# Issuing the stores of the recurrences from POOL's queue instead of SP's in a hybrid HGRN2 / Mamba-2 layer

## The chip, the cores and the metric

The kernel runs on one core of a Trainium2 chip. The core has five engines that work side by side, each through its own instructions in order: TensorE (PE, matrix products; its weight loads are shown as PEld), VectorE (DVE), ScalarE (ACT), GpSimd (POOL) and SyncE (SP). SP computes nothing; it issues DMA transfers. POOL computes and can issue DMA transfers too. An issued transfer runs on the core's 16 DMA engines; its issuer goes on to its next instruction. Engines wait for each other and for transfers through semaphores.

The metric is device time in microseconds (us), the median of several runs. Less is better.

## What is computed

One layer of a decoder trunk for two request groups that share all weights: a prompt of 1024 tokens from a zero state, and 8 sample tokens with states of their own. All data is fp32, the model width is 1024.

```python
h = rmsnorm(x, norm1_w)
q, f, i, g, z, xbc, dt = split(h @ w_in)            # 1024 -> 6672 columns
# A: HGRN2, 8 heads, key and value dim 128
f = lb + (1 - lb) * sigmoid(f); k = 1 - f; q = silu(q)
S = f_t * S + k_t v_t;  o = q_t S                   # chunked over the prompt; one step per sample
o_a = rmsnorm(o) * silu(g)
# B: Mamba-2 SSD, 16 heads of 64, 2 B/C groups, state 128
X, B, C = silu(causal_conv4(xbc)); dt = softplus(dt + bias)
S = exp(A dt) * S + dt X B;  y = C S + D X
y = rmsnorm(y * silu(z))
x = x + concat(o_a, y) @ w_out                      # 2048 -> 1024
gate, val = split(rmsnorm(x, norm2_w) @ w_up)       # 1024 -> 2 x 2816
x = x + (silu(causal_conv3(gate)) * val) @ w_down
y = rmsnorm(x, final_norm_w)
```

Returned are y and the new states of both groups: HGRN states, SSM states, the last rows before each convolution.

## The kernel before, in words

A token column set holds 1024 prompt tokens and 8 sample tokens (NT = 1032) and is cut into three chunks of 344 columns for the input projection. Each fp32 product is made of three: a tile is split into a high part (rounded on ScalarE) and a low part (the rest, by a subtraction on VectorE), and TensorE adds high·high, high·low and low·high. So a weight tile of 128 columns, 512 KB, is loaded by SP into `ws` (two buffers, L182), cast on ScalarE (L183) and subtracted on VectorE (L184).

The input projection is a list of **jobs** (`in_job`), one for each 128 columns, each of 72 matrix products. Between the products of the jobs the program interleaves the work of the recurrences, by `drive(stream, weight, name)`: the stream yields numbers, and for each so many matrix products of the jobs are issued. Weights are loaded two jobs ahead. **TensorE's order is written out by hand** (`manual_schedule` for PE alone); the order of VectorE, ScalarE, POOL and SP is made when the program is built, by a scheduler that estimates when each instruction can run. Each of these engines then works in that fixed order.

In order of time:

- norm of the input, first columns of B and C, dt (about 0 to 100 us);
- SSM recurrence of group 0, `ssd(0)`, then of group 1, in 8 chunks of 128 tokens. `ssd_front` (L519) loads rows of decay sums (`csb`), makes B's transpose (`bt`), X·dt (`xdt`, L543, VectorE) and its decayed form (`xde`, L544, POOL). `ssd_back` (L549) makes the output and the next state: `ecs` (loaded; L563 on VectorE), the decayed state (L568, POOL), its sum with the new part (L569, VectorE), output sums (L579, L582). TensorE needs the state of L569 for the next chunk's product `yo`;
- `ssm_decode` (L614), one step for the samples, in two halves of four samples for each of eight head pairs: it loads B and C rows (`Bb`, `Cb`) and the state `Sd` (two buffers), scales it on ScalarE (L627), multiplies on VectorE (L628), adds (L629), **stores the state (L630)**, multiplies by C on POOL (L631) and reduces on VectorE (L632), then updates the sample columns (L633);
- `ssm_gate` (L642): jobs z, whose columns gate the SSM output; `tail` (L679) scales the four tiles of a group (L683) and **stores them in the scratch tensor `mix_d` (L684)**;
- eight HGRN heads (`head`, L810). The sample rows of v are **stored in scratch `vd_d` (L824)** and loaded back as `vb`, broadcast; the sample states `Sh` are loaded, updated on VectorE and POOL (L833 to L835) and **stored (L836)**, and used by TensorE (`od`). Levels of products with `f`, `k`, `q`, `v` follow (L853 to L857), the prompt state is **stored (L948)**, the output is normed (L983, POOL) and **stored in `mix_d` (L988)**;
- beside them, rows before the convolution go out through a buffer `csr` (**L698, L699**), and one DRAM to DRAM copy (**L700**); the prompt's SSM state goes out through `so` (**L597**);
- the output projection: the rows of `mix_d` are loaded back as `ml` (`mix_load`, L1001), split (L998 on ScalarE, L999 on VectorE), multiplied; evictions in ScalarE (L1038) or VectorE (L1040). Residual input columns `xs` are loaded by `residual_load` (L756), in buffers that `vb` uses too;
- from about 1000 us on: second norm, up projection, down projection, final norm. None of the changed lines lies there.

All loads and all stores named here are issued by SP, in one order. POOL issues only nine small loads (`vec`, L139) at the start.

Changed and calling functions:

Of the kernel before, what the change touches and what calls it, by code (L numbers as in the profile page):

```python
# [20 lines left out]
NT = T + ND  # L21
# [29 lines left out]
def hybrid_layer(  # L51
# [9 lines left out]
    V, A, G, PE, SP = nc.vector, nc.scalar, nc.gpsimd, nc.tensor, nc.sync  # L61
# [27 lines left out]
    def bank(s, tag="mx"):  # L89
        return psmx.tile([P, 512], F32, tag=tag, bufs=NBANK[tag], name=nm(s))  # L90
# [237 lines left out]
    mix_d = dram.tile([16, P, NT], F32, name="mix_d")  # L328
# [96 lines left out]
    for i in range(9):  # L425
        n = P if i < 8 else ND
# [164 lines left out]
    def ssm_state_out(g):  # L591
        ps = bank("sT")
        for i in range(4):
            PE.transpose(ps[:, i * P:(i + 1) * P], S[g][:, i * P:(i + 1) * P], ident)
        so = half("so")
        V.tensor_copy(so, ps)
        SP.dma_start(ssm_prompt[0, 0, g * 8:(g + 1) * 8].rearrange("(i h) p n -> (h p) i n", h=2),  # L597
                     so.rearrange("p (i n) -> p i n", n=P))

    def d4(t):  # L600
        return t.rearrange("p (b n) -> p b n", n=P)
# [12 lines left out]
    def ssm_decode(g, i):  # L614
        j = g * 4 + i
        xdd = small.tile([P, 2, ND], F32, tag="xdd", name=nm("xdd"))
        xdec = Xg[g][i][:, T:NT]
        V.tensor_tensor(xdd[:, 0, :], xdec, ddb[:, 0, j, :], op=ALU.mult)
        for b0 in (0, 4):
            bs = slice(b0, b0 + 4)  # L620
            Bb, Cb = tl("d", "Bb")[:, :512], tl("d", "Cb")[:, :512]
            for t_, r in ((Bb, 2 * g), (Cb, 2 * g + 1)):
                fetch(t_, bc_d[r, bs].rearrange("b n -> (b n)").unsqueeze(0).to_broadcast([P, 512]))
            Sd = tl("ld", "Sd")
            fetch(d4(Sd), state_ssm[0, bs, 2 * j:2 * j + 2].rearrange("b h p n -> (h p) b n"))
            for b in range(4):
                A.activation(d4(Sd)[:, b, :], d4(Sd)[:, b, :], AF.Copy, scale=ddb[:, 1, j, b0 + b:b0 + b + 1])  # L627
            V.tensor_tensor(d4(Bb), d4(Bb), cb(xdd[:, 0, bs]), op=ALU.mult)  # L628
            V.tensor_tensor(Sd, Sd, Bb, op=ALU.add)  # L629
            SP.dma_start(ssm_sample[0, bs, 2 * j:2 * j + 2].rearrange("b h p n -> (h p) b n"), d4(Sd))  # L630
            G.tensor_tensor(Cb, Sd, Cb, op=ALU.mult)  # L631
            V.tensor_reduce(xdd[:, 1, bs], d4(Cb), axis=mybir.AxisListType.X, op=ALU.add)  # L632
        V.scalar_tensor_tensor(xdec, xdec, d_bc[:, j:j + 1], xdd[:, 1, :], op0=ALU.mult, op1=ALU.add)  # L633
# [8 lines left out]
    def ssm_gate(g):  # L642
        acc = []

        def z_job(i):
            j = g * 4 + i

            def begin():
                if i == 0:
                    acc.append(tl("g", "gacc"))  # L650
                if g:
                    ssm_decode(1, i)
                elif i < 2:
                    ssm_decode(0, i + 2)

            def evict(c, cs, ps):
                Y = Xg[g][i][:, cs]
                sz = tl("z", "sz")[:, :CH]
                A.activation(sz, ps, AF.Silu)
                V.tensor_tensor(Y, Y, sz, op=ALU.mult)  # L660
                if i == 0:
                    A.activation(acc[0][:, cs], Y, AF.Square)
                else:
                    A.activation(sz, Y, AF.Square)
                    (V if g or i == 3 else G).tensor_tensor(acc[0][:, cs], acc[0][:, cs], sz, op=ALU.add)
                if i == 3:
                    after(36 + 14 * g, lambda: rstd(c))
            in_job(f"z{j}", OFF_Z + j * P, evict, begin=begin)

        def rstd(c):  # L670
            cs = chunks[c]
            ps = bank("ms", "nx")
            mm(ps[:, :CH], ones, acc[0][:, cs])
            rstd_of(acc[0][:, cs], tl("z", "nt")[:, :CH], ps[:, :CH], 512)

            if c == NCH - 1:
                tail()

        def tail():  # L679
            for i in range(4):  # L680
                j = g * 4 + i
                Y = Xg[g][i][:, :NT]
                V.scalar_tensor_tensor(Y, Y, col("sn", j), acc[0][:, :NT], op0=ALU.mult, op1=ALU.mult)  # L683
                SP.dma_start(mix_d[8 + j], Y)  # L684

        for i in range(4):
            z_job(i)

    def ssm_conv_state():
        for j0 in range(0, XT, 4):  # L690
            yield
            ps = bank("l11", "nx")
            for j in range(4):
                PE.transpose(ps[:11, j * P:(j + 1) * P], last11[:, j0 + j, :], ident)
            csr = keep.tile([16, 512], F32, tag="csr", bufs=1, name=nm("csr"))
            V.tensor_copy(csr[:11, :512], ps[:11, :])
            cl = slice(j0 * P, (j0 + 4) * P)
            SP.dma_start(cs_prompt[0, 0, :, cl], csr[0:3, :512])  # L698
            SP.dma_start(cs_sample[0, :, 2, cl], csr[3:11, :512])  # L699
        SP.dma_start(cs_sample[0, :, 0:2, :], state_conv_ssm[0, :, 1:3, :])  # L700

    def ssd(g):
        parts = {}
# [36 lines left out]
    vd_d = dram.tile([H, ND, P], F32, name="vd_d")  # L740
# [69 lines left out]
    def head(h, t):  # L810
        f, k, q, v, sg = (t[n] for n in ("f", "k", "q", "v", "sg"))
# [9 lines left out]
            A.copy(vt[hf], ps)  # L821
        vd = small.tile([ND, P], F32, tag="vd", name=nm("vd"))
        V.tensor_copy(vd, dps[:ND, :P])
        SP.dma_start(vd_d[h], vd)  # L824
        V.tensor_tensor(qb[:, :, 0:ND], eye8, q[:, T:NT].unsqueeze(2).to_broadcast([P, ND, ND]), op=ALU.mult)
        Sds = []
        for b0 in (0, 4):
            bs = slice(b0, b0 + 4)
            ds = slice(T + b0, T + b0 + 4)
            Sd, vb = tl("ld", "Sh"), tl("d", "vb")[:, :512]  # L830
            fetch(d4(Sd), state_hgrn[0, bs, h].rearrange("b k v -> k b v"))
            fetch(vb, vd_d[h, bs].rearrange("b n -> (b n)").unsqueeze(0).to_broadcast([P, 512]))
            G.tensor_tensor(d4(vb), d4(vb), cb(k[:, ds]), op=ALU.mult)  # L833
            V.tensor_tensor(d4(Sd), d4(Sd), cb(f[:, ds]), op=ALU.mult)
            G.tensor_tensor(Sd, Sd, vb, op=ALU.add)  # L835
            SP.dma_start(hgrn_sample[0, bs, h].rearrange("b k v -> k b v"), d4(Sd))  # L836
            Sds.append(d4(Sd))


# [80 lines left out]
        for b in range(ND):  # L920
            g = b % 4
# [12 lines left out]
        Sprev, before = None, []  # L934
        for hf in range(2):
# [4 lines left out]
            for i in range(4):  # L940
# [4 lines left out]
                    V.scalar_tensor_tensor(SS[hf][:, blk[i]], Sprev, Tc[:, hf * 4 + i:hf * 4 + i + 1], ps[:, blk[i]],  # L945
                                           op0=ALU.mult, op1=ALU.add)
                Sprev = SS[hf][:, blk[i]]
        SP.dma_start(hgrn_prompt[0, 0, h], Sprev)  # L948
        dps = bank("odp", "nx")
        mm(dps[:, :ND], odr, selod)  # L950
        od = small.tile([P, 3, ND], F32, tag="dsq", name=nm("od"))
# [6 lines left out]
        for hf in range(2):  # L958
            oh = sg[:, hb[hf]]
            ps = bank("o")  # L960
            for i in range(4):
                n = hf * 4 + i
# [22 lines left out]
        oh = sg[:, T:NT]  # L985
        V.scalar_tensor_tensor(oh, od[:, 0, :], col("hn"), oh, op0=ALU.mult, op1=ALU.mult)
        V.tensor_tensor(oh, oh, od[:, 1, :], op=ALU.mult)
        SP.dma_start(mix_d[h], sg[:, :NT])  # L988


    def split(src, hi, lo):
# [409 lines left out]
    for c in (3, 0, 1, 2):  # L1401
# [4 lines left out]
        for t0 in range(cs.start, cs.stop, P):  # L1406
            n = min(P, cs.stop - t0)
# [49 lines left out]
```

## Time and profile before

| | |
|---|---|
| median of 3 runs | 1786.03 us (1785.04 to 1788.24) |
| profiled execution | 1782.61 us, span 1780.9 us |
| granted clock of TensorE, mean | 0.991 |
| TensorE busy | 1725.4 us, 97% |
| VectorE busy | 1119.3 us, 63% |
| ScalarE busy | 817.5 us, 46% |
| transfers issued by SP (hardware queue) | 179.80 MB, 32.3% of 16 engines' span |
| transfers issued by POOL (software queue) | 0.10 MB |

The profile is of one execution. Busy time counts instructions on an engine; issuing a DMA isn't counted, but shown in the timeline. A row of the waits reads "engine, line <- what released it: us in total, times, longest". A row of the timeline reads start, length (us), engine, line, operation, output<-inputs, shape, count, and in brackets the idle time before it and what ended it; rows with a count above 1 are merged, and a length is then that of the whole. A row of the stage table reads stretch, its length, then busy time of PE, PEld, DVE, ACT and POOL with counts, the granted clock of TensorE (1.00 is full), the DMA engines' share and GB/s.

### The profile page before, as it was taken

To read this page: it belongs to the slowest core of one execution; us is meant where nothing else is said; L and a number is where in the kernel's file an instruction comes from. 1 tells how busy PE (TensorE), PEld (TensorE's weight loads), DVE (VectorE), ACT (ScalarE), POOL (GpSimd) and SP (SyncE) were. 2 spreads that over 40 slices of the span, in tenths; PEclk is the share of its full clock that TensorE was granted. 3 is DMA by queue.
4 is the path that set the end of the run, shared out by engine and by line. 5 is a ranking of instruction groups with operands and counts; after the bars stand their busy time and mean duration, and the time that the engine had idled before them with its cause. 6 is when DMAs were issued, how large, how long until landed. Compare 5 with 4: busy or idle time off the path is not lost. (4 is left out here: it accounts for less than half of the span.)

```text
span 1780.9 us, 38506 instructions
## 1 busy us (share of the span) xinstructions
PE 1725.4 (97%) x16143; PEld 1675.6 (94%) x16143; DVE 1119.3 (63%) x2011; ACT 817.5 (46%) x1464; POOL 405.3 (23%) x415
## 2 busy tenths in 40 slices
PE   7999899999999999999999978999999999999998
PEld 6998799999999999999899978999999999999997
DVE  6667966575564565458645768666666666445545
ACT  7677688455554454545333435334333344111114
POOL 2113331220110111011000364554445542000001
PEclk9999999999999999999999998999999999999999
DMA  4144634642221222234334432222222225422212
GB/s 154 39 126 126 189 106 132 184 137 98 87 66 51 86 73 78 58 109 155 101 108 133 135 90 72 72 72 78 82 91 72 72 84 203 152 81 90 97 61 96
DMA packets 218019, 182.34 MB, mean 102 GB/s; under 512 B 13388, under 2 KB 195158, under 8 KB 217830
## 3 DMA queue, kind: packets, MB, share of 16 engines
q1 hardware_dynamic: 217558, 179.80, 32.3%
q8 instruction: 126, 2.06, 0.5%
q14 instruction: 47, 0.39, 0.1%
q0 software_dynamic: 288, 0.10, 0.0%
HBM read 141.53 MB, written 38.52 MB: 101 GB/s over the span
## 5 line engine op out<-in xcount | busy, mean ns | idle before, releaser
L93 PE MATMUL mm<-hh,wh 128*128 128x344 f32 x1248 | 405.3, 325 | 0.3 <-issue 0.2
L93 PE MATMUL mm<-hl,wh 128*128 128x344 f32 x1248 | 404.5, 324 | 0.0
L93 PE MATMUL mm<-hh,wl 128*128 128x344 f32 x1248 | 402.0, 322 | 0.0
L93 PEld LDWEIGHTS mm<-hh,wh 128*128 128x128 f32 x1248 | 235.0, 189 | 3.9 <-issue 2.6
L93 PEld LDWEIGHTS mm<-hl,wh 128*128 128x128 f32 x1248 | 235.2, 189 | 2.4 <-issue 0.9
L93 PEld LDWEIGHTS mm<-hh,wl 128*128 128x128 f32 x1248 | 235.3, 189 | 2.2 <-issue 1.5
L183 ACT CAST wh<-ws 128x1024 fp32r<-128x1024 f32 x96 | 100.5, 1047 | 242.8 <-PE dn L93 135.3
L93 PE MATMUL ub<-ul,wh 128*128 128x258 f32 x704 | 200.4, 285 | 4.3 <-DVE ul L1144 4.3
L93 PE MATMUL ub<-uh,wh 128*128 128x258 f32 x704 | 200.3, 285 | 2.0 <-ACT uh L1143 2.0
L93 PE MATMUL ub<-uh,wl 128*128 128x258 f32 x704 | 200.2, 284 | 0.0
L93 PE MATMUL dn<-ah,wh 128*128 128x256 f32 (+1 forms) x640 | 181.1, 283 | 1.2 <-DVE x L1387 1.2
L93 PE MATMUL dn<-al,wh 128*128 128x256 f32 (+1 forms) x640 | 180.6, 282 | 0.0
L93 PE MATMUL dn<-ah,wl 128*128 128x256 f32 (+1 forms) x640 | 180.2, 282 | 0.0
L184 DVE TENSOR_TENSOR wl<-ws,wh 128x1024 fp32r<-128x1024 f32 x96 | 126.4, 1317 | 72.4 <-ACT wh L183 71.4
L93 PE MATMUL mm<-mh,wh 128*128 128x258 f32 x512 | 147.7, 288 | 11.2 <-DVE x L1040 8.3
L93 PE MATMUL ua<-ul,wh 128*128 128x258 f32 x528 | 149.4, 283 | 0.9 <-DVE ul L1144 0.9
L93 PE MATMUL ua<-uh,wh 128*128 128x258 f32 x528 | 149.2, 283 | 0.0
L93 PE MATMUL ua<-uh,wl 128*128 128x258 f32 x528 | 148.4, 281 | 0.0
L93 PE MATMUL mm<-ml,wh 128*128 128x258 f32 x512 | 145.8, 285 | 0.7 <-DVE ml L999 0.7
L93 PE MATMUL mm<-mh,wl 128*128 128x258 f32 x512 | 145.9, 285 | 0.0
L93 PEld LDWEIGHTS ub<-ul,wh 128*128 128x128 f32 x704 | 134.5, 191 | 5.0 <-DVE ul L1144 5.0
L93 PEld LDWEIGHTS ub<-uh,wh 128*128 128x128 f32 x704 | 134.0, 190 | 2.5 <-ACT uh L1143 2.5
(347 smaller groups left out, 3942.8 us busy)
## 6 DMA issues: line engine op xcount, KB each, us to landing
ws<-in_w_in_dram SPq DMA_DIRECT2D x52, 512.0 KB
ws<-in_w_up_dram SPq DMA_DIRECT2D x44, 512.0 KB
ws<-in_w_out_dram SPq DMA_DIRECT2D x24, 512.0 KB
act_d<-val SPq DMA_DIRECT2D x22, 516.0 KB
al<-act_d SPq DMA_DIRECT2D x22, 516.0 KB
ws<-in_w_down_dram SPq DMA_DIRECT2D x22, 512.0 KB
ml<-mix_d SPq DMA_DIRECT2D x48, 172.0 KB
csb<-cs_d SPq DMA_DIRECT2D x32, 256.0 KB
```

Source lines behind the costliest of these rows:

```text
L93: PE.matmul(out, lhsT, rhs, start=start, stop=stop)
L183: A.copy(wh[:, :n], ws[:, :n])
L184: V.tensor_tensor(wl[:, :n], ws[:, :n], wh[:, :n].bitcast(F32), op=ALU.subtract)
```

## The change

Ten statements that store results now use POOL's queue (`G.dma_start`) instead of SP's (`SP.dma_start`). They issue 73 transfers. All loads stay with SP; so do the stores of the second half of the kernel. Source, destination and size of each transfer are unchanged. As the scheduler orders the engines anew, instructions on VectorE, ScalarE, POOL and SP change places too, mainly between 140 and 380 us and near 840 us; TensorE's order is the same.

```diff
 def ssm_state_out(g):
-        SP.dma_start(ssm_prompt[0, 0, g * 8:(g + 1) * 8].rearrange("(i h) p n -> (h p) i n", h=2),
+        G.dma_start(ssm_prompt[0, 0, g * 8:(g + 1) * 8].rearrange("(i h) p n -> (h p) i n", h=2),
                      so.rearrange("p (i n) -> p i n", n=P))
 def ssm_decode(g, i):
             V.tensor_tensor(Sd, Sd, Bb, op=ALU.add)
-            SP.dma_start(ssm_sample[0, bs, 2 * j:2 * j + 2].rearrange("b h p n -> (h p) b n"), d4(Sd))
+            G.dma_start(ssm_sample[0, bs, 2 * j:2 * j + 2].rearrange("b h p n -> (h p) b n"), d4(Sd))
             G.tensor_tensor(Cb, Sd, Cb, op=ALU.mult)
 def tail():
-                SP.dma_start(mix_d[8 + j], Y)
+                G.dma_start(mix_d[8 + j], Y)
 def ssm_conv_state():
-            SP.dma_start(cs_prompt[0, 0, :, cl], csr[0:3, :512])
-            SP.dma_start(cs_sample[0, :, 2, cl], csr[3:11, :512])
-        SP.dma_start(cs_sample[0, :, 0:2, :], state_conv_ssm[0, :, 1:3, :])
+            G.dma_start(cs_prompt[0, 0, :, cl], csr[0:3, :512])
+            G.dma_start(cs_sample[0, :, 2, cl], csr[3:11, :512])
+        G.dma_start(cs_sample[0, :, 0:2, :], state_conv_ssm[0, :, 1:3, :])
 def head(h, t):
-        SP.dma_start(vd_d[h], vd)
+        G.dma_start(vd_d[h], vd)
...
-            SP.dma_start(hgrn_sample[0, bs, h].rearrange("b k v -> k b v"), d4(Sd))
+            G.dma_start(hgrn_sample[0, bs, h].rearrange("b k v -> k b v"), d4(Sd))
...
-        SP.dma_start(hgrn_prompt[0, 0, h], Sprev)
+        G.dma_start(hgrn_prompt[0, 0, h], Sprev)
...
-        SP.dma_start(mix_d[h], sg[:, :NT])
+        G.dma_start(mix_d[h], sg[:, :NT])
```

## The prediction

> **What bounds the kernel now.** I read the page's busy table first, then TensorE's waits from 100 to 1000 us (the stretch in which all moved stores lie), then a table by stage.
>
> ```profile
> PE 1725.4 (97%) x16143; PEld 1675.6 (94%) x16143; DVE 1119.3 (63%) x2011; ACT 817.5 (46%) x1464; POOL 405.3 (23%) x415
> ```
> ```profile
> PE xp L541 <- DVE ecs L563: 3.0, 2, 2.2
> PE mm L93 <- ACT x L1038: 2.8, 1, 2.8
> PE yo L93 <- DVE S L569: 2.6, 1, 2.6
> PE a L93 <- DVE q L854: 2.5, 1, 2.5
> ```
> ```profile
> 500.00:800.00 300.00, 299.10 (x3997) 289.16 (x3996) 165.37 (x300) 149.91 (x237) 41.95 (x30) 1.00 0.26 77
> 206.20:209.40 3.20, 2.96 (x10) 2.21 (x10) 3.20 (x5) 1.28 (x4) 2.35 (x2) 0.50 0.17 45
> 411.00:414.20 3.20, 2.94 (x132) 2.83 (x133) 2.58 (x5) 0.94 (x3) 0.00 (x0) 0.50 0.59 167
> 851.30:854.50 3.20, 3.20 (x50) 2.91 (x49) 1.70 (x4) 3.08 (x10) 0.00 (x0) 0.50 0.17 52
> ```
>
> TensorE is the bound: 97% busy, and from 500 to 800 us 299.10 of 300 us. TensorE's order is the same in both kernels, so the change can only fill or open gaps. The four longest waits in the stretch make 10.9 us. The last three rows (columns: span, PE, PEld, DVE, ACT, POOL, then granted clock) show a second price: after each of the waits of 2.6, 2.5 and 2.8 us the granted clock is 0.50 for some 3.2 us, so 1.6 us is lost on top; after the wait of 2.2 us it isn't. POOL, where the stores go, is 23% busy. None of TensorE's waits here ends on a DMA or on SP, so a shorter SP queue helps only through VectorE or ScalarE.
>
> **What leaves SP.** 73 stores: 16 of the SSM decode states (L630), 16 of the HGRN decode states (L836), 16 of gate rows (L684, L988), 8 HGRN states (L948), 8 value rows (L824), 7 of convolution rows (L698 to L700), 2 SSM states (L597). SP issues in order, so a store that waits for its producer holds back the loads behind it:
>
> ```profile
> SPq L836 <- POOL Sh L835: 62.8, 16, 6.9
> SPq L630 <- DVE Sd L629: 28.2, 12, 7.4
> ```
>
> These waits go, but most are late for nobody: the loads behind them fetch weights two jobs ahead, and TensorE waits for no weight. What is late next in SP's queue is a weight load waiting for its buffer. I count a gain only where a TensorE gap follows from such a load or from the order that changes with it.
>
> **What a store costs on POOL.** No store was issued there; the small loads of the start are the nearest rows.
>
> ```profile
> L139 POOL DMA_DIRECT2D vrows<-in_norm_w_dram x2 | 1.2, 598 | 0.8 <-POOLq L1445 0.8
> L139 POOL DMA_DIRECT2D vrows<-in_ffn_conv_w_dram x1 | 0.6, 550 | 0.0
> L139 POOL DMA_DIRECT2D vrows<-in_hgrn_norm_w_dram x1 | 0.5, 511 | 0.0
>   DMA to landing us min/median/max: 4.3/5.6/6.1
> ```
> ```profile
> 147.76 3.23 POOL L544 TENSOR_TENSOR xde<-xdt,dec 128x512 f32<-128x512 f32 x1 [1.08 <-DVE xdt L543]
> 151.95 2.51 POOL L631 TENSOR_TENSOR Cb<-Sd,Cb 128x512 f32<-128x512 f32 x2
> 160.21 1.04 POOL L544 TENSOR_TENSOR xde<-xdt,dec 128x512 f32<-128x512 f32 x1 [5.74 <-DVE xdt L543]
> ```
>
> One row of 128 floats took 511 ns, 66 rows 550 ns: 0.5 us and about 0.6 to 1 ns a row. A decode-state store has 512 rows of 512 bytes, so 0.8 to 1.0 us; I take 1.0. The low end is 0.5 us. The high end is 3.2 us, what a POOL instruction of 1.04 us became when VectorE worked beside it. 73 times 1.0 us is 73 us on an engine idle for 1375 us, so POOL's total is no matter; what stands behind a store is. At L630 that is L631 (Cb), for which VectorE's L632 waits. Landing is 5.6 us after issue by these rows; on SP the value rows were stored and loaded back within 1.9 us:
>
> ```profile
> 385.51 0.31 SPq L824 DMA_DIRECT2D vd_d<-vd  x1
> 387.40 1.04 SPq L175 DMA_DIRECT2D vb<-vd_d  x2
> 404.46 3.93 SPq L684 DMA_DIRECT2D mix_d<-xbc  x4
> ```
> ```profile
> 407.23 1.28 ACT L799 ACT_TABLE_LOAD   x1 [2.12 <-DMA mix_d<-xbc]
> ```
>
> **Stage 1, the SSM recurrence of group 0 (100 to 230 us).** The change also moves instructions on VectorE and ScalarE.
>
> ```profile
> 148.80 1.29 DVE L629 TENSOR_TENSOR Sd<-Sd,Bb 128x512 f32<-128x512 f32 x2
> 153.28 0.69 DVE L632 TENSOR_REDUCE xdd<-Cb 128x4 f32<-128x512 f32 x1 [3.19 <-POOL Cb L631]
> 155.10 0.68 DVE L563 TENSOR_TENSOR ecs<-yo,ecs 128x512 f32<-128x512 f32 x1
> 176.56 0.68 DVE L629 TENSOR_TENSOR Sd<-Sd,Bb 128x512 f32<-128x512 f32 x1
> 184.37 0.67 DVE L632 TENSOR_REDUCE xdd<-Cb 128x4 f32<-128x512 f32 x1
> 184.96 1.16 DVE L629 TENSOR_TENSOR Sd<-Sd,Bb 128x512 f32<-128x512 f32 x1
> 186.04 1.53 DVE L628 TENSOR_TENSOR Bb<-Bb,xdd 128x512 f32<-128x512 f32 x1
> 188.76 0.69 DVE L632 TENSOR_REDUCE xdd<-Cb 128x4 f32<-128x512 f32 x1 [1.18 <-POOL Cb L631]
> 205.62 0.67 DVE L569 TENSOR_TENSOR S<-S,st 128x512 f32<-128x512 f32 x1
> ```
> ```profile
> 168.16 0.40 ACT L627 ACTIVATE Sd<-Sd,ddb 128x128 f32<-128x128 f32 x1 [0.80 <-DMA Sd<-in_state_ssm_dram]
> ```
>
> At 153 us TensorE waits 2.2 us for L563, which stands behind the reduce L632 that waits 3.19 us for POOL. In the new order L569 and L563 stand ahead of that reduce, so the gap closes. But the two stores put 2.0 us of POOL time before the second reduce, VectorE reaches the next chunk's L543 no sooner, and TensorE meets it there: I count this as nothing. What counts is when L569 at 205.62 ends, for which TensorE waits 2.6 us. Out of the stretch before 189 us go 0.68 + 0.67 + 1.16 + 1.53 + 0.69 us of decode work and the wait of 1.18: 5.9 us. Of this, two L629 (1.3), a wait of store plus Cb less one L629 (1.0 + 1.3 - 0.6 = 1.7) and a reduce (0.6) come back ahead of the next L563: 3.6. On ScalarE the scaling of the second decode leaves the front of a chunk (0.40 + 0.80 = 1.2 us). I take off 0.5 for the second reduce behind the longer POOL queue: 5.9 - 3.6 + 1.2 - 0.5 = **3.0 us** sooner. Bounds: a gain of 9 (all gaps of the stage and the slow clock go), a loss of 6 (stores at the high end, rival B).
>
> **Stage 2, the first heads (385 to 415 us).** TensorE's 2.5 us there comes from VectorE's in-order work, whose order stays: no gain. A loss is possible. ScalarE waited at 407.23 for the first gate-row store to land, because the next head's q goes into its buffer, 2.8 us after issue. At 5.6 us it starts 2.8 us later, and the copies of the head's level behind it some 1.4 us; TensorE was idle in part of that. I take **+1.0 us**, between 0 and 2.8. The Trainium skill, page "DMA: Bandwidth & Descriptors", section "Latency and other measured facts", gives about 1 us to the first byte from POOL and 0.6 from SP. By that the store would land only 0.4 us later and the sum would be an estimate of 1.0 us better; the rows show 5.6 against 1.9 us, though in the crowded start.
>
> **Stage 3, the last head (838 to 855 us).**
>
> ```profile
> 846.65 0.48 ACT L998 CAST mh<-ml 128x344 fp32r<-128x344 f32 x1 [3.52 <-DMA ml<-mix_d]
> 848.78 0.48 ACT L998 CAST mh<-ml 128x344 fp32r<-128x344 f32 x1 [1.01 <-DMA ml<-mix_d]
> 849.68 0.36 ACT L1038 COPY x<-mm 128x258 f32<-128x258 f32 x1
> ```
> ```profile
> 841.34 0.38 SPq L836 DMA_DIRECT2D out_dram<-Sh  x1
> 843.63 1.45 SPq L175 DMA_DIRECT2D ml<-mix_d  x3
> ```
>
> TensorE's 2.8 us end with the eviction L1038, which stands behind casts that wait for rows of the mixer. The third of the three loads left SP near 844.6 and was cast at 848.78, some 4 us later; the group had stood behind stores and residual loads that wait for POOL. Without the stores, and with two of these loads ahead of one residual load, I place the last load that L1038 has to await (five casts precede it in the new order) near 843.8. With 3 to 4 us to its cast, L1038 ends near 848.6 instead of 850.0: 1.5 us, and with a gap near 1.3 us the slow clock (1.6) should not follow. That is **3.1 us**. Bounds: 4.4 gain, 1 loss (the residual loads still wait for POOL's L835, now behind a store).
>
> ```profile
> 854.87 0.64 PE L93 MATMUL od<-Sh,qb 128*32 128x128 f32 x16
> ```
>
> **Hidden.** Stores L836, L824, L948, L988 of heads 1 to 6: TensorE is busy throughout, and the HGRN state, stored at 841 us in head 7, is used at 855, 14 us later. If landing exceeded that, weights behind the value-row load would be next. L700 moves to an idle POOL at the start, L597 and L698/L699 are a few: nothing.
>
> **Sum.** -3.0 + 1.0 - 3.1 = -5.1 us. The profiled run took 1782.61 us (span 1780.9), 3.4 below the median of 1786.03; from it 1777.5, on the runs' median **1781**.
>
> **Rivals.**
> A, hidden anyway: VectorE in stage 1 is the bound whatever its order, so it keeps its time, and stage 3 gains only 1 to 2 us. For it: 153.04 of 200 us busy from 100 to 300 us. Time 1785.
>
> ```profile
> 100.00:300.00 200.00, 190.90 (x1310) 175.55 (x1309) 153.04 (x256) 160.09 (x317) 50.80 (x51) 0.99 0.46 135
> ```
>
> B, slower: the store holds POOL longer than 1.0 us. Two stores stand before the second reduce of each decode, and two decodes lie on stage 1's path, so each extra us costs 4 there and 1 in stage 3. The sum turns at -5.1 + 5(x - 1) = 0, x = 2.0 us. At the high end, 3.2 us, it is +5.9: 1792. For it: POOL's instructions do stretch beside VectorE (1.04 to 3.23). Against: the loads of the start took 0.5. The Trainium skill, page "SBUF — State Buffer", section "Who interferes with whom", says that VectorE's two-port instructions lock POOL out of writing descriptors; no store is in this trace to show it, and this rule speaks against the change.
>
> C, larger gain: all four waits and the slow clocks behind them go, 10.9 + 4.8 us: 1770.
>
> **How the numbers follow.** Forecast 0.42, A 0.25, B 0.25, C 0.08. A measurement of this kernel tells about 0.2% (3.6 us) from no change. The forecast's own range is 1776 to 1785, so 0.35 of its 0.42 is faster and 0.07 same; C adds 0.08 to faster; A is same but for 0.03 slower; B is slower. Faster 0.43, same 0.29, slower 0.28. The range of 1773 to 1793 leaves out most of C and B's far end.
>
> **What would show it.** Right: POOL's L630 stores near 1.0 us each; no TensorE wait over 1 us at L563 near 153; the 203 us wait ending about 3 us sooner; the wait for L1038 near 847 below 1.5 us with no 0.50 clock behind it. Wrong: stores over 2.0 us, VectorE's waits for L631 far above before, or gaps near 410 us that grew by more than 2 us.

## The result and the profile after

The changed kernel takes 1797.54 us (median of 6 runs, 1794.63 to 1799.52) against 1785.16 us before (6 runs on the same chip): a ratio of **1.0069, 95% interval 1.0054 to 1.0085**, 12.4 us slower. The prediction was 1781 us, faster. The profiled execution of the changed kernel took 1795.5 us, its span is 1793.8 us. Each of the two profiled executions, this one and that of before (1782.61 us), is 2 to 3 us quicker than its kernel's median, so their difference, 12.9 us, is near the 12.4. Over all later comparisons the median of the kernel before was 1786.2 to 1787.2 us, some 4 us above its trace. Stages are read from the traces, sizes from the ratios.

The busy table of after, and TensorE's waits from 100 to 1000 us (sum, times, longest):

```profile
PE 1730.5 (96%) x16143; PEld 1680.8 (94%) x16143; DVE 1123.8 (63%) x2011; ACT 816.8 (46%) x1464; POOL 449.3 (25%) x488
```
```profile
PE mm L93 <- ACT sz L659: 4.4, 2, 3.5
PE a L93 <- DVE q L854: 3.6, 1, 3.6
PE yo L93 <- ACT Sd L627: 3.3, 1, 3.3
PE xp L541 <- DVE ecs L563: 2.4, 1, 2.4
...
PE mm L93 <- ACT x L1038: 1.6, 1, 1.6
```

POOL gained 44 us of work, TensorE is still the bound. But the longest waits are new ones. At the top stands one that the kernel before doesn't have at all: TensorE waits for ScalarE's eviction L659 of the z jobs, the gates of group 1. Since TensorE's order is the same, each of its products can be compared with itself. The changed kernel's product starts 2.2 us sooner at 156 us, 3.6 us later at 230, 3.9 at 335, 11.3 at 370, 13.3 at 450, 14.1 at 840, 12.3 at 900 and 13.1 at 1700 us. **More than half of the loss, 7.8 us, arises between 335 and 385 us**, 7.4 of it before 370 us, in a stretch that the prediction doesn't speak of. A table by stretch (span, then PE, PEld, DVE, ACT, POOL, granted clock, DMA share, GB/s), first before, then after:

```profile
335.00:376.00 41.00, 41.00 (x262) 41.00 (x261) 21.98 (x38) 17.38 (x45) 7.90 (x6) 1.00 0.67 203
```
```profile
335.00:387.00 52.00, 47.62 (x285) 46.95 (x285) 26.29 (x44) 17.76 (x45) 15.29 (x15) 0.93 0.61 178
363.50:370.30 6.80, 5.22 (x18) 5.22 (x19) 3.37 (x5) 3.49 (x8) 3.59 (x4) 0.50 0.44 124
```

Before, TensorE was busy for all of these 41 us. After, it waits 4.4 us, and around the wait of 3.5 us the clock is 0.50 for 6.8 us: 5.22 us of work at half speed, another 2.6. That is 7.0 of the 7.8 us.

**The ring of a z job.** In each z job of group 1 a decode of two halves runs (`ssm_decode(1, i)`). The main rows of SP and VectorE in one job before, by time (the loads of `Bb`, `Cb` and of the first half's `Sd` are left out):

```profile
344.19 0.37 SPq L182 DMA_DIRECT2D ws<-in_w_in_dram  x1
344.80 0.40 SPq L630 DMA_DIRECT2D out_dram<-Sd  x1
...
349.01 0.38 SPq L175 DMA_DIRECT2D Sd<-in_state_ssm_dram  x1
352.30 0.69 DVE L628 TENSOR_TENSOR Bb<-Bb,xdd 128x512 f32<-128x512 f32 x1 [1.05 <-DMA Bb<-bc_d]
353.03 0.69 DVE L629 TENSOR_TENSOR Sd<-Sd,Bb 128x512 f32<-128x512 f32 x1
355.18 0.69 DVE L632 TENSOR_REDUCE xdd<-Cb 128x4 f32<-128x512 f32 x1 [1.46 <-POOL Cb L631]
355.79 1.22 DVE L184 TENSOR_TENSOR wl<-ws,wh 128x1024 fp32r<-128x1024 f32 x1
357.03 0.37 SPq L182 DMA_DIRECT2D ws<-in_w_in_dram  x1
```

and the same job after, with POOL's store:

```profile
352.02 0.38 SPq L182 DMA_DIRECT2D ws<-in_w_in_dram  x1
352.89 0.78 POOL L630 DMA_DIRECT2D out_dram<-Sd  x1 [2.75 <-DVE Sd L629]
...
359.85 0.38 SPq L175 DMA_DIRECT2D Sd<-in_state_ssm_dram  x1
361.09 0.69 DVE L628 TENSOR_TENSOR Bb<-Bb,xdd 128x512 f32<-128x512 f32 x1 [2.12 <-DMA Bb<-bc_d]
362.20 0.69 DVE L629 TENSOR_TENSOR Sd<-Sd,Bb 128x512 f32<-128x512 f32 x1 [0.42 <-ACT Sd L627]
365.30 0.69 DVE L632 TENSOR_REDUCE xdd<-Cb 128x4 f32<-128x512 f32 x1 [2.41 <-POOL Cb L631]
365.90 1.22 DVE L184 TENSOR_TENSOR wl<-ws,wh 128x1024 fp32r<-128x1024 f32 x1
367.14 0.38 SPq L182 DMA_DIRECT2D ws<-in_w_in_dram  x1
```

Read as a ring: SP issues the weight load, and behind it the loads of the next decode. When they land, VectorE multiplies (L628) and adds (L629), POOL makes the product, VectorE reduces (L632). Behind the reduce, in VectorE's order, stands L184, which frees the weight buffer; only then can SP issue the next weight load, and behind that the next decode's loads. Before, the ring took 357.03 - 344.19 = 12.84 us. TensorE needs less, some 11.3 us for the 72 products of a job (262 products in the 41.00 us above), so the ring was the slower of the two already; that TensorE was busy all the same fits weights being loaded two jobs ahead. After, the ring took 367.14 - 352.02 = 15.12 us. The 2.28 us: the second L628 starts 9.07 us into the ring and not 8.11 (+0.96, the loads land later); L629 follows 1.11 and not 0.73 us behind it (+0.38); L632 follows L629 after 3.10 and not 2.15 us (+0.95, POOL issues the store first).

The loads land later although SP issues them sooner, right behind the weight load. At the same place in the ring, for 3.3 us, the DMA engines were fully taken both times, but moved 306 GB/s before (345.87 to 349.17 us, the store being ahead of these loads in SP's queue) and 220 GB/s after (353.70 to 357.00 us, when the store had not begun to move). That this is why they land later is read from the two stretches; no run tests it, and the second L628 is late by 1.32 us in the ring ahead of this one and by 0.08 in the one behind it.

Beside it runs a second way. The reload of the second half of `Sd` needs the slot whose store is under way. Before, SP issued that store directly behind the weight load and the reload 4.21 us after it (344.80 to 349.01); after, POOL issues it and the reload goes out 6.96 us later (352.89 to 359.85). ScalarE's scaling L627 of that half follows, in four parts. **ScalarE's order has changed here too**: after, the weight part L183 (for which VectorE's L184 waits as well) and the eviction L659 stand behind three of the four parts; before, they stood ahead of them. The rows of ScalarE, before and then after, with TensorE's row that waits for the eviction:

```profile
352.90 1.04 ACT L183 CAST wh<-ws 128x1024 fp32r<-128x1024 f32 x1
353.85 0.44 ACT L659 ACTIVATE sz<-mm 128x344 f32<-128x344 f32 x1
354.19 1.27 ACT L627 ACTIVATE Sd<-Sd,ddb 128x128 f32<-128x128 f32 x4
```
```profile
362.76 0.98 ACT L627 ACTIVATE Sd<-Sd,ddb 128x128 f32<-128x128 f32 x3 [0.59 <-DMA Sd<-in_state_ssm_dram]
363.65 1.03 ACT L183 CAST wh<-ws 128x1024 fp32r<-128x1024 f32 x1
364.58 0.45 ACT L659 ACTIVATE sz<-mm 128x344 f32<-128x344 f32 x1
365.08 0.66 PE L93 MATMUL mm<-hh,wh 128*128 128x344 f32 x1 [3.52 <-ACT sz L659]
```

TensorE's long wait is for ScalarE, not for a weight. The eviction L659 starts 12.56 us into the ring and not 9.66 (364.58 - 352.02 and 353.85 - 344.19). Of these 2.9 us, 0.95 arise because the first half's L627 starts later (at 360.50, before at 351.72; its load lands later too), 0.6 are the wait for the reload, and the other 1.4 are the new order, in which three parts of L627 and an L662 stand ahead of it. The waits of the stretch, before (335 to 376 us), then after (339 to 387):

```profile
SPq L175 <- DMA out_dram<-Sd: 8.3, 5, 3.4
ACT Sd L627 <- DMA Sd<-in_state_ssm_dram: 3.5, 1, 3.5
DVE xdd L632 <- POOL Cb L631: 8.5, 6, 1.5
```
```profile
SPq L175 <- DMA out_dram<-Sd: 16.7, 4, 5.6
ACT Sd L627 <- DMA Sd<-in_state_ssm_dram: 17.6, 6, 6.5
DVE xdd L632 <- POOL Cb L631: 11.3, 5, 2.4
```

What had to be found out is which of these causes carries the loss: the slot, POOL's time ahead of the product, the new order of the other engines, or any of the other 57 stores.

### The profile page after: what moved, and what is told of

It reads as the page before. It is cut to its first block, busy times and chain, and to the rows that moved or that the text cites. A ratio compares the mean times of both kernels' runs of the same rounds, so it can differ in the third digit from the quotient of the medians.

```text
span 1793.8 us, 38574 instructions
## 1 busy us (share of the span) xinstructions
PE 1730.5 (96%) x16143; PEld 1680.8 (94%) x16143; DVE 1123.8 (63%) x2011; ACT 816.8 (46%) x1464; POOL 449.3 (25%) x488
## 4 chain that ended last, share of the span: by engine, by line
PE 78%; DVE 7%; DMA 5%; ACT 5%; issue 3%; POOL 1%; SPq 1%; DVEq 0%; POOLq 0%; ACTq 0%
PE mm L93 31%; PE ub L93 14%; PE dn L93 14%; PE ua L93 10%; DMA csb<-cs_d 2%; PE a L93 2%; PE o L93 1%; ACT csb L530 1%; DMA Sd<-in_state_ssm_dram 1%; PE kv L93 1%; DMA ml<-mix_d 1%; DVE xbc L334 1%; DVE wl L184 1%; SPq L175 1%; ACT L531 1%
## 5 line engine op out<-in xcount | busy, mean ns | idle before, releaser
L183 ACT CAST wh<-ws 128x1024 fp32r<-128x1024 f32 x96 | 100.5, 1047 | 248.6 <-PE dn L93 135.2
L184 DVE TENSOR_TENSOR wl<-ws,wh 128x1024 fp32r<-128x1024 f32 x96 | 125.8, 1311 | 72.0 <-ACT wh L183 71.2
```

The costliest lines, as they stand in the source:

```text
L183: A.copy(wh[:, :n], ws[:, :n])
L184: V.tensor_tensor(wl[:, :n], ws[:, :n], wh[:, :n].bitcast(F32), op=ALU.subtract)
```

## The experiments

Ratios are to the kernel before, run beside each kernel on the same chip. The three rings from 331 to 383 us are given from SP's weight loads: 12.94, 12.84 and 13.82 us before, 15.20, 15.12 and 14.81 after.

### Which stores: L630 alone, all but L630

```diff
# L630 alone: the only line that differs from before
-            SP.dma_start(ssm_sample[0, bs, 2 * j:2 * j + 2]...)
+            G.dma_start(ssm_sample[0, bs, 2 * j:2 * j + 2]...)
# all but L630: the changed kernel with that line put back to SP
```

> Only the 16 stores of the decode states at L630 go out on POOL's queue; the other 57 stay in SP's. Theory T1 (the loss sits in the decode of the state-space heads: the store of Sd lands later on POOL's queue, so SP reloads the slot later, ScalarE waits at L627 and its evictions behind it are late): this kernel has the whole loss or more of it, because the changed kernel gains 2.4 us near 850 us from other stores: 8 to 15 us above the kernel before (1793 to 1800 us), with gaps of 2.5 to 3.5 us at the L659 evictions between 335 and 385 us. Rival R1 (each of the 73 moved stores costs about the same, by POOL's time or by the write traffic): 16/73 of 12.4 us, that is about 2.7 us (1788 us). Rival R2 (the new order of VectorE's and SP's work in the first recurrence, 100 to 230 us, is the main loss): about 4 us, all of it before 230 us and nothing at 335 to 385 us.

> The 57 other stores go out on POOL's queue; the 16 of L630 stay in SP's. T1: no loss at 335 to 385 us; what is left is the gain of about 2.4 us near 850 us and the losses of 1.1 to 1.6 us near 415 and of 1.3 us near 587 us, in sum 1784 to 1788 us, no difference from the kernel before or a small one. R1: 57/73 of 12.4 us, about 9.7 us above the kernel before (1795 us). R2: between 0 and 8 us above it, the rest of the loss.

L630 alone: 1798.03 us, **1.0057** (1.0039 to 1.0075); rings 14.08, 14.61, 14.93. All but L630: 1788.88 us, **1.0007** (0.9995 to 1.0019); rings 14.02, 13.10, 14.06. The 16 stores of the decode states carry the loss, the other 57 none that can be told from nothing. A cost shared evenly by all stores is out.

### Which of the 16: group 1 alone, group 0 alone

```diff
# group 1 alone; group 0 alone has SP and G the other way round
-            SP.dma_start(ssm_sample[...
+            (G if g else SP).dma_start(ssm_sample[...
```

> Only the 8 stores of L630 of group 1 (issued at 335 to 385 us) on POOL's queue; the 8 of group 0 (100 to 240 us) and the other 57 in SP's. From the traces the gates of group 1 lost 7.3 us and the stretch before them 3.9 us in the changed kernel: 6 to 8.5 us above the kernel before (1793 to 1795 us) and no new gap before 335 us. Rival (the loss of the gates is carried over from a disorder in the first recurrence): under 3 us.

> Only the 8 stores of L630 of group 0 (100 to 240 us) on POOL's queue, those of group 1 and the other 57 in SP's. From the run with group 1 alone, which has the whole loss (1.0060): 0 to 4 us above the kernel before (1786 to 1790 us), all of it between 160 and 240 us, and rings of 13 to 14 us at 335 to 385 us as before. Rival (the new order of VectorE and SP that these 8 stores bring with them is what costs): 6 us or more.

Group 1 alone, 8 stores: 1797.24 us, **1.0060** (1.0043 to 1.0076); rings 14.42, 14.64, 14.81. Group 0 alone: 1787.82 us, **1.0005** (0.9996 to 1.0014); rings 13.20, 12.88, 14.05. So the eight stores in the gates of group 1 bring the whole loss. In VectorE's order 17 places hold another line than before with group 1 alone, 124 in the changed kernel; group 0 alone has 94 and costs nothing that shows. The new order of the first recurrence is therefore not the cause. The new wait is there with group 1 alone too: from 335 to 387 us TensorE waits 4.2 us for L659, 3.1 at the longest.

The new order in the gates isn't ruled out by these runs. Group 1 alone changes 17 places of ScalarE's order as well, all of them from 349 to 383 us. All six kernels with group 1's stores of L630 on POOL's queue have L183 and L659 behind three parts of the second half's L627 in the last two of the three rings, as shown above; all others have them ahead of at least three. The order is made anew with each edit, so no run separates the two. The kernel below with both other causes removed keeps the new order and stands at 1.0011: the order alone costs no more than that, but how much of the other two causes' cost needs it stays open.

### The slot: three buffers for the states

To make room the tag `d` is narrowed and `bcr` shares the place of `csr`. The tag `ld` serves the sample states `Sh` of the heads too.

```diff
-        "z": (384, 4), "s": (HW, 11), "d": (HW, 4), "ld": (512, 2),
+        "z": (384, 4), "s": (HW, 11), "d": (512, 4), "ld": (512, 3),
-        bcr = small.tile([ND, 2 * P], F32, tag="bcr", bufs=1, name=nm("bcr"))
+        bcr = keep.tile([16, 512], F32, tag="csr", bufs=1, name=nm("bcr"))[:ND, :2 * P]
```

> All 73 stores on POOL's queue as in the changed kernel, but the tag of the decode states has three slots and not two, so a reload waits for the store of three halves before. (The room comes from bcr, which shares csr's place, used at other times, and from the unused ends of the tag d.) T1 by the slot: the waits of SP at L175 for a store of Sd go from 16.7 us between 339 and 385 us to under 5, ScalarE's at L627 from 17.6 to under 6, and the 7.3 us of that stretch come back: 1786 to 1791 us. R3 (not the slot but POOL's time in front of L631, or the loads of Bb and Cb, whose slots stay four): no more than 2 us come back, 1795 to 1798 us.

> The control of the run with the third slot: all stores in SP's queue as before, three slots for the decode states. T1: the kernel before waits for the slot at SP 12.5 us in the whole run, most of it beside other work, so 0 to 3 us faster than before (1782 to 1786 us); the third slot is worth far more on POOL's queue (6 to 10 us) than on SP's. R3: the same on both, within 1.5 us.

With the stores on POOL's queue: 1792.85 us, **1.0026** (1.0017 to 1.0035); with all of them in SP's: 1784.62 us, **0.9984** (0.9971 to 0.9997). So the slot matters, and by the medians more on POOL's queue (0.43 points back) than on SP's (0.16). But neither theory was right: the gain is between the two, and the rings stayed long, 14.78, 14.61 and 15.17 us (13.71, 13.11 and 13.98 with the stores in SP's queue). In the stretch (335 to 383 us) SP waits half as long for a store, and ScalarE and TensorE as long as ever:

```profile
SPq L175 <- DMA out_dram<-Sd: 8.3, 2, 5.5
ACT Sd L627 <- DMA Sd<-in_state_ssm_dram: 16.5, 6, 6.1
PE mm L93 <- ACT sz L659: 5.9, 2, 3.3
DVE xdd L632 <- POOL Cb L631: 11.2, 6, 2.4
```

In this profile what came back lies before 335 us: from there to 385 us TensorE loses 7.4 us, as against 7.8 in the changed kernel, so where the third slot's gain lies isn't shown. The theory that the slot alone does it fell here. The last row points to the way by POOL.

### POOL's time: the store behind the product, and POOL's time without a store

```diff
# the store behind the product
+            G.tensor_tensor(Cb, Sd, Cb, op=ALU.mult)
             G.dma_start(ssm_sample[0, bs, 2 * j:2 * j + 2]..., d4(Sd))
-            G.tensor_tensor(Cb, Sd, Cb, op=ALU.mult)
# POOL's time alone: the kernel before, with scr a spare tile
-            G.tensor_tensor(Cb, Sd, Cb, op=ALU.mult)
+            G.tensor_copy(scr, Sd[:16]); G.tensor_tensor(Cb, Sd, Cb, op=ALU.mult)
```

> All 73 stores on POOL's queue, as in the changed kernel, but at L630/L631 POOL first makes the product Cb and issues the store of Sd behind it (the two lines are swapped). Theory T2, formed after the run with the third slot left ScalarE's wait of 16.5 us and the gaps of 5.9 us at 335 to 383 us in place: VectorE's L632 waits for the product, the weight part L184 stands behind L632, SP's next weight load and the loads of the next job stand behind L184; the 0.78 us that POOL needs to issue the store (with the step to the product 0.97 us) lie in that ring, which grew from 12.84 to about 15.1 us a job. T2: VectorE's wait at L632 falls from 2.43 back to about 1.5 us, the ring to 14.0 to 14.3 us, TensorE's gaps before L659 to under 3 us, and 3 to 6 us of the 12.4 come back (1791 to 1794 us). Rival T3 (not POOL's time but the store's lost place in SP's queue and its late landing): the store lands 1.3 us later still, the slot comes free later, 1797 to 1800 us.

> All stores stay in SP's queue; POOL copies 16 rows of Sd to a spare tile ahead of each product Cb, 16 copies of an estimated 0.8 to 1.0 us, about what the issue of a store takes there. No transfer moves. T2: the ring grows by about 0.9 us a job, TensorE's gaps at 335 to 385 us appear, and with the scheduler's answer in the first recurrence the time is 3 to 9 us above the kernel before (1790 to 1796 us). T3: within 1.5 us of the kernel before.

The store behind the product: 1796.89 us, **1.0063** (1.0049 to 1.0077), nothing back that can be told, and close to what T3 had. POOL's time alone: 1792.65 us, **1.0033** (1.0020 to 1.0046); its copies took 0.60 us in the median (the store's issue 0.78), and the rings 13.91, 13.67 and 14.24 us. So POOL's time ahead of the product does cost by itself, about half of the loss, though not all of it in the ring: in the trace TensorE loses 3.9 us from 335 to 385 us, and 2.5 at the wait for L1038 near 850 us, where this edit touches nothing. And yet taking POOL's time away gave nothing. The waits of the kernel with the store behind the product (335 to 387 us) say why:

```profile
DVE xdd L632 <- POOL Cb L630: 9.9, 7, 1.5
SPq L175 <- DMA out_dram<-Sd: 22.3, 4, 6.3
DVE wl L184 <- ACT wh L183: 4.6, 3, 1.8
```

VectorE's wait for the product is back at 1.5 us, as expected. But the store goes out behind the product and lands later, SP reloads the slot later, and now L184 waits for ScalarE's L183, which stands behind the late half of L627. The rings are 15.48, 15.10 and 15.70 us. Both ways round the ring had grown by about 2 us; the third slot eased one, and the swap took away one and lengthened the other.

### Both at once

The two edits above together: three slots, and the product ahead of the store.

> All 73 stores on POOL's queue, with both suspects taken away at once: POOL makes the product Cb first and issues the store of Sd behind it, and the decode states have three slots. Theory T4, formed from the ring of a job at 335 to 385 us (12.84 us before, 15.12 in the changed kernel, 14.61 with the third slot alone, 15.10 with the swap alone): two ways round are both longer by about 2 us, one by POOL's issue ahead of the product, one by the slot of Sd (SP's reload at 7.66 to 8.96 us of the ring instead of 4.4 to 4.8, then ScalarE's L627 and L183, then L184), so that taking away one leaves the other. T4: the ring falls to 13.2 to 13.9 us, TensorE's gaps before L659 to under 2.5 us, and the time to 1786 to 1790 us, 0.0 to 0.2% above the kernel before. Rival T5 (what makes the loads of Bb and Cb land 0.5 to 1 us later beside a store on POOL's queue is the main cause): the ring stays at 14.3 us or more and the time at 1791 us or more.

1789.46 us, **1.0011** (1.0002 to 1.0020). Rings 14.10, 13.28 and 14.47 us; the profiled execution was the slowest of its eleven, and its rings are a little longer than the theory had them, TensorE's wait too:

```profile
SPq L175 <- DMA out_dram<-Sd: 4.9, 1, 4.9
DVE xdd L632 <- POOL Cb L630: 8.7, 6, 1.5
PE mm L93 <- ACT sz L659: 3.5, 2, 2.3
```

In that trace TensorE still loses 4.9 us from 335 to 385 us. That both together take most of the loss away rests on the medians.

### The other 57 stores with three slots, and the stores at the end of the heads

> The 57 other stores on POOL's queue, the 16 of L630 in SP's, and three slots for the decode states. If the parts add up (other stores +0.07%, third slot with the stores in SP's queue -0.16%): 1783 to 1787 us, 0 to 0.15% under the kernel before. If POOL's queue makes the sample states Sh wait for their slot too (16 stores at L836 use the same tag), the third slot is worth more here, 1780 to 1783 us.

> Three slots for the decode states, and of the 73 stores only the 16 at the end of the heads (L948 and L988) on POOL's queue. The orders of VectorE and ScalarE are those of the run with the third slot alone (0.9984 of the kernel before). If the gain of 2.4 us seen near 850 us comes from these stores and is real: 1780 to 1784 us (0.9965 to 0.9985). If it was the scatter of single profiles: as the third slot alone, 1783 to 1786 us, and then none of the 73 stores is better off on POOL's queue.

The 57 other stores on POOL's queue, with three slots: 1786.96 us, **1.0000** (0.9989 to 1.0011); rings 13.74, 12.87 and 14.04 us. Only L948 and L988 on POOL's queue, with three slots: 1783.14 us, **0.9985** (0.9971 to 0.9998), the same as the third slot alone (a time that lies in both ranges); rings 13.65, 13.74 and 14.56 us. The shorter wait near 850 us that the changed kernel shows is therefore no gain of these 16 stores: with them alone on POOL's queue TensorE's wait for L1038 is 3.1 us, as long as before. That the other 41 gain anything isn't seen in any run.

Taken together, the 16 stores of L630 on POOL's queue cost this much beside the same kernel with them in SP's queue (ratios divided, each good to some 0.15 to 0.2 points; the column with three slots is set against 1.0000):

| | two slots | three slots |
|---|---|---|
| store ahead of the product | 1.0062 (1.0069 / 1.0007) | 1.0026 |
| product ahead of the store | 1.0056 (1.0063 / 1.0007) | 1.0011 |

The swap alone takes back 0.06 points, the slot alone 0.36, both 0.51 of 0.62. With the slot free the swap is worth 0.15 points, barely clear of the noise, and with two slots nothing that can be told; that these two differ isn't shown.

### Another queue: the stores on ScalarE's

```diff
-            SP.dma_start(ssm_sample[0, bs, 2 * j:2 * j + 2]...)
+            A.dma_start(ssm_sample[0, bs, 2 * j:2 * j + 2]...)
```

> The 16 stores of L630 leave SP's queue too, but for ScalarE's queue; the other 57 stay in SP's, two slots. POOL's time is untouched. What it tells: on POOL's queue a store issued behind no load moved 1.35 us after its issue, and one with SP's burst of loads ahead of it 4.1 us after (issued at 352.89, moving from 357.04 to 359.12), which kept the slot of Sd. If that is what any second queue gives (the store loses its place among SP's transfers), the stores issued here beside SP's burst land late as well, SP's waits at L175 for a store of Sd stay at 12 us or more in the whole run, and the time is 1789 to 1797 us. If the late landing belongs to POOL's queue (its descriptors and 4096-byte packets), the stores here land about as in the kernel before, and the loss is only what ScalarE's evictions wait behind L629: 1786 to 1791 us.

1789.24 us, **1.0013** (1.0000 to 1.0026); rings 14.96, 14.00 and 13.97 us in its profile. SP waits as long for the slot as in the changed kernel (24.2 us in the whole run, 5.2 at the longest; before 12.5 and after 25.1).

So the late landing isn't POOL's alone: on both second queues tried, a store issued beside SP's burst of loads moves late. The DMA table of two stretches shows it, in the changed kernel (store issued by POOL at 352.89) and in this one (by ScalarE at 347.78). First the changed kernel from 353.7 to 357.0 us, and then from 357.0 to 359.2:

```profile
DMA packets 1013, 0.73 MB, mean 220 GB/s; under 512 B 26, under 2 KB 870, under 8 KB 1013
...
DMA packets 714, 0.81 MB, mean 370 GB/s; under 512 B 48, under 2 KB 492, under 8 KB 714
q0 software_dynamic: 80, 0.26, 29.3%
```

and the kernel with ScalarE's queue from 347.8 to 350.2 us, and then to 353.1:

```profile
q1 hardware_dynamic: 735, 0.38, 67.2%
...
q1 hardware_dynamic: 624, 0.63, 77.5%
q10 hardware_dynamic: 527, 0.26, 30.1%
```

q1 is SP's queue; in the changed kernel's first stretch it moves all 0.73 MB. In the first stretch of each the second queue moves nothing, though the store's issue began before it; its 0.26 MB come in the second, while SP's loads go on (in the second stretch with ScalarE's queue q1 moves 0.63 MB). In SP's queue the store stood directly behind the weight load, ahead of the decode's loads; on a queue of its own it falls behind what is already on the way. But here no POOL time lies on the other way round, L183 and L659 stand ahead of at least three parts of the second half's L627 as before, and the loss is about a quarter of that on POOL's queue.

### What stays open

About 0.1 points are left with both causes removed, and their place isn't settled: in the profile of that kernel one of the three rings has the second L628 1.3 us later than before (9.50 us into the ring, 8.18 before), the other two not. Single profiles scatter (the kernel before alone ran from 1780.5 to 1794.7 us), and the rings of one execution don't order all kernels as their medians do: the kernel with ScalarE's queue has longer rings in its profile than the one with POOL's time alone, and the smaller loss, and the kernel with only L948 and L988 moved has rings as long as POOL's time alone and no loss. What TensorE loses from 335 to 385 us in each trace, its products compared with those of before, goes better with the stores: 7.4 to 9.8 us in the five kernels with group 1's stores on POOL's queue and at most one cause removed, 4.9 with both removed, 4.3 on ScalarE's queue, 3.9 with POOL's time alone, 2.7 with all but L630, and -0.6 to 0.8 in the other four. POOL's time alone (+0.33%) and ScalarE's queue (+0.13%) add up to 0.46, and L630 on POOL's queue costs 0.57%; that is the same within the intervals, and the sum wasn't tested further.

**A version that beats both kernels** is the one with three slots and all stores in SP's queue: 1784.62 us, 0.16% under the kernel before (0.03 to 0.29%).

## Why the prediction was wrong

**What bounds the kernel**: right. TensorE's order is the same, and only gaps and the slow clock behind them count.

**Hidden, the step that failed.** The prediction counted 16 stores at L630 and followed them only in stage 1, where 8 of them lie. The other 8, in the gates of group 1, were neither among the stages nor in the list of what is hidden. The sentence that closed that door was that most of SP's waits "are late for nobody": it looked for gains from waits that go, in stretches where TensorE already had gaps, and at 335 to 376 us TensorE was 41.00 of 41.00 us busy. That full row said that there is nothing to gain there; it didn't say how much slack the ring behind it had. Its weight loads, 12.84 to 13.82 us apart, beside the 11.3 us that a job's products take, would have: none. Both costs were in the prediction's own terms, 1.0 us of POOL ahead of L631 and a later landing, and neither was put into that ring. TensorE still waits for no weight there; it waits for the eviction L659, which stands on ScalarE behind the late loads of `Sd`, in an order made anew. The eight stores of these gates are the 0.6%.

**A store on POOL**: the mechanism right, the size a little high. Predicted 1.0 us for a decode-state store; the minimum, median and maximum of L630 in ns, and the time to landing in us:

```profile
L630 POOL DMA_DIRECT2D out_dram<-Sd x16: 757/781/848, 152.3 to 383.2; - x16
DMA to landing us min/median/max: 2.7/3.7/6.9
```

Landing, put at 5.6 us, was 3.7 in the median, and up to 6.9 (1.6 us in the median for the small value rows of L824). Rival B, the only one on the side where the result fell, needed stores of over 2.0 us; none took more than 0.85. Its sign came true and its mechanism didn't. The rule of the Trainium skill that stood beside it (page "SBUF — State Buffer", section "Who interferes with whom") would, if it acts within the issue, show as stretched issues; the 16 of L630 spread from 757 to 848 ns, and of the rest one gate row of L684 took 957 ns where the median is 545. Whether an instruction of the kind that the rule names stood beside any of them isn't shown.

**Stage 1, -3.0 us**: wrong in sign. The gap at 153 us closed as said, and TensorE was 2.2 us ahead at 156. But at 165.9 the same wait for L563 came back with 2.4 us, `yo` waited 3.3 us for ScalarE's L627, and at 230 us TensorE was 3.6 us behind. The working moved busy times about on VectorE and ScalarE and left SP out: with the stores gone, the load of the next `Bb` waits in SP's queue for L629 (17.3 us from 130 to 232 us, a wait that L630 had before), and the decay rows stand behind it. ScalarE's waits for those rows in that stretch, before and then after:

```profile
ACT csb L530 <- DMA csb<-cs_d: 7.2, 4, 3.1
```
```profile
ACT csb L530 <- DMA csb<-cs_d: 19.7, 5, 7.7
```

The queue was blocked at its head as before, only by a load and not by a store. Timed by itself (group 0 alone) this costs 0.05%, within the scatter.

**Stage 2, +1.0 us**: the size right by luck, the reason wrong. TensorE's wait for L854 grew from 2.5 to 3.6 us, and it is 3.2 to 3.6 us in all six kernels with all 57 other stores on POOL's queue and 2.5 to 2.7 in the rest, but for 3.1 with L630 on ScalarE's. But the gate row isn't the cause: the first of them landed at most 3.0 us after its issue (stored at 417.54, ScalarE on at 420.56), and 2.8 before (404.46 and 407.23). The sentence that the prediction took from the Trainium skill (page "DMA: Bandwidth & Descriptors", section "Latency and other measured facts"), 0.4 us later, was nearer than its own 2.8. VectorE was late before any gate row was stored: its L854 starts 12.81 us later than before (410.22 and 397.41), the one that TensorE waits for just as much (423.12 and 410.31), while TensorE's products at 400 us are 11.7 us late. Of these 1.1 us, 0.58 come from one L853, before and then after:

```profile
395.72 1.77 DVE L853 TENSOR_TENSOR k<-k,f 128x512 f32<-128x512 f32 x1
```
```profile
407.95 2.35 DVE L853 TENSOR_TENSOR k<-k,f 128x512 f32<-128x512 f32 x1
```

After, POOL's L833, L835 and two stores of L836 lie beside it (405.1 to 410.8 us); before, the two stores were SP's and POOL was done at 396.9. The prediction had called L836 hidden. That it is POOL's work that stretches VectorE's here is read from the overlap, no run took it away alone.

**Stage 3, -3.1 us**: right in the two traces (2.8 to 1.6 us, and no 0.50 clock, 2.4 us in all), but no gain to rely on: with L948 and L988 alone on POOL's queue the wait is 3.1, and with all 57 and three slots 2.8. In kernels that move no store of that stretch it comes out anywhere from 0.8 us (L630 on ScalarE's queue) to 5.3 (POOL's time alone), so a change from 2.8 to 1.6 shows nothing of the stores. Where it does come, in the kernel with all but L630, stage 2 takes it back, and that kernel stands at 1.0007.

**Rival A** (hidden, 1785 us) describes the 57 other stores well. What it missed is the same as the forecast.

## What to carry to other kernels

Before a transfer is moved to another queue, list for each of its copies what waits for it to land (a slot's reload above all) and what stands behind its issue on the new engine, and put both into the shortest ring that passes there; a stretch in which the bounding engine is fully busy may have no slack behind it, which the spacing of its loads, set against the time of one job, shows and the busy share doesn't. A store that leaves a queue gives up its place ahead of the loads behind it, and if those share its slots they can wait longer, not shorter. When two lengthened ways end at the same instruction, removing one may give part of the loss back or nothing (here 0.36 and 0.06 of 0.62 points, both 0.51): test both together before a cause is acquitted. And compare the order of every engine at the place of the loss: an edit to one queue changed ScalarE's order there as well.

## What the runs showed of the hardware that was not expected

- A store of 256 KB on a second queue, POOL's or ScalarE's, began to move late beside SP's burst of loads: POOL's issued at 352.89 us from 357.0 on, ScalarE's issued at 347.78 from about 350.5 on, in both cases with SP's loads still going on. With no load ahead it began 1.4 us after the issue on POOL's queue (issued at 348.04) and 0.9 on ScalarE's (343.70). Of the decode states none landed on POOL's queue earlier than 2.7 us after the issue.
- SP's burst (a weight tile, `Bb`, `Cb` and `Sd`) ran at 220 GB/s with the engines fully taken (353.7 to 357.0 us), where the same place of the ring before, with the store ahead of the decode's loads in SP's queue and a share of 1.05, had 306 GB/s; the next 2.2 us after it reached 370 GB/s.
- The issue of the same store takes 0.78 us on POOL, 0.38 on ScalarE and 0.39 on SP. On POOL's queue it went as 80 packets, on ScalarE's as 527.
- Around the wait of 3.5 us at 365 us the granted clock was 0.50 for 6.8 us, twice as long as at the waits of about 2.5 us before. But at the wait of 3.6 us for L854, near 424 us, it was 0.50 for only some 3.4 us (424.9 to 428.4 us: 0.51), so the length of the wait alone doesn't set it.
